# Sums over partitions for the adaLN blocks: ones-products and DRAM rows replaced by block transposes, row sums and one small product

## The chip, the cores and the metric

One Trainium2 chip, of which the kernel uses one core. The metric is the device time of one launch in microseconds; lower is better. The engines of the core run side by side and wait for each other through semaphores: TensorE (PE, with its weight loads as PEld) multiplies, VectorE (DVE), ScalarE (ACT) and GpSimd (POOL) work element by element, and SyncE (SP) issues every DMA of this kernel from one queue, in order.

## The reference

Two layers of a diffusion backbone for 640 tokens (128 context, 512 latent) of 1024 features, all in float32. Each layer mixes tokens through three branches (gated MLP, attention, RWKV-7), merges them, and then runs an MLP; each half is modulated by six vectors of 1024 values for each of two conditionings (the context's and the latent's):

```python
mod = (jax.nn.silu(cvec) @ P['w_ada'][l] + P['b_ada'][l])[:, None, :]
sh1, sc1, g1, sh2, sc2, g2 = jnp.split(mod, 6, axis=-1)
h = x * (1 + sc1) + sh1
...
x = _layer_norm(ALPHA * x + g1 * mixed, P['ln1_g'][l], P['ln1_b'][l])
h = x * (1 + sc2) + sh2
f = jnp.square(jax.nn.relu(h @ P['w_up'][l])) @ P['w_down'][l]
x = _layer_norm(ALPHA * x + g2 * f, P['ln2_g'][l], P['ln2_b'][l])
```

The change concerns `mod`: for each layer a product of two rows of 1024 with a 1024 x 6144 matrix, 24 MB of weights read once.

## The kernel before

Big products are made from float32r parts: a weight block of 128x512 is loaded (`raw`), ScalarE copies it to `hi`, VectorE subtracts to get `lo` (`split`, L240 to L242), and three products (hi hi, hi lo, lo hi) stand for one of float32. There are three buffers for each of `raw`, `hi` and `lo`, so the splits run a little ahead of the products.

The `mod` matrix is cut into 12 blocks of 512 columns a layer; block `cb` belongs to the vector `cb // 2`. The first four blocks of layer 0 are done at the start by TensorE (`ada_first`). The other 20 go through `ada_block` (L290): for each of eight k-tiles it loads 128x512 weights (`wada`) and adds weights times silu(c) to an accumulator of 128x512 for each of the two conditionings, on VectorE (L306, L308), or, for the six blocks of layer 0 that run before the MLP, half of it on ScalarE and GpSimd (L302, L304). What is left is a sum over the 128 partitions. There, at L309 to L322, two products with a column of ones (L315) put each conditioning's sum as one row of 512 on one partition, 0 or 64, of a PSUM bank; the bias is loaded as a row (L314), added on VectorE (L318), and the row goes to DRAM (L319). The two gate vectors (2 and 5) are later read from there as rows, broadcast to all partitions (`res_rows`). The shifts and scales (0, 1, 3, 4) are wanted with features on partitions: after the second block of a vector, one DMA for each conditioning gathers 1024 single values into the tile `mod0`, `mod1`, `mod3` or `mod4` of shape [128, 8, 2] (L322).

`ada_block` is a generator; each `next` does one k-tile. Two blocks run at the start, before the RWKV projections (`EARLY`); four in the gates and merge of layer 0, three steps for each step of those (L389 to L392); and 14 (two of layer 0, twelve of layer 1) in layer 0's MLP, three steps behind each up projection of 128 features and each down projection of 256 columns (L1216, L1243). The MLP of layer 1 has none. In the MLP the weights of a step lie in a tile `P` with two buffers, which the bias rows share; the accumulator is `acc`. Layer 0's gate vector 5 (the two first of the 14 blocks) is read before the last quarter of the same MLP, and layer 1's shift and scale 0 and 1 at its end.

Instructions are written in the order of this code, and a planner places them in each engine's queue when the program is built, by a simulated timeline; on the chip every engine runs its queue in that order.

Of the kernel before, what the change touches and what calls it, by code (L numbers as in the profile page):

```python
# [11 lines left out]
F32 = mybir.dt.float32  # L12
# [11 lines left out]
KT = D // 128  # L24
# [6 lines left out]
# emission order of the units' stages: those of the prologue, then those of a period  # L31
# [15 lines left out]
class Two(list):  # L47
    """Two PSUM banks for the first cut tokens and the others."""
    cut = HALF

    def of(self, h, x):
        """Part h of the tokens of x."""
        return x[:, self.cut:NTOK] if h else x[:, 0:self.cut]
# [5 lines left out]
class Net:  # L59
# [67 lines left out]
    # ---- weights: 256 KB blocks, each split into two float32r parts that sum to it exactly  # L127
    def wsplit(self, src, extra=False):
        """[128, 1024] of weights as two blocks of 512 columns."""
        return [self.whalf(src[:, 512 * i:512 * i + 512], extra) for i in range(2)]  # L130
# [15 lines left out]
    # out[128 features, 640 tokens] in two halves; w: (hi, lo) column slices, x: lists of (hi, lo)  # L146
    def mm_k(self, ps, w, k, x):
        """The products of one of eight k-tiles."""
# [16 lines left out]
    def fm_blocks(self, srcs, xs, first=0, pre=()):  # L165
        """The products of successive weight blocks; the first three by parts of the tokens when first."""
# [22 lines left out]
    # token-major: out[tt] = x[tt].T @ w, 256 columns, w blocks of 4 k-tiles  # L189
# [20 lines left out]
    def tm_last(self, srcs, xs, slots):  # L210
        """The last two column blocks, one token tile after the other; yields each tile's [128, 512]."""
# [24 lines left out]
    def ev(self, ps, t):  # L236
        """Pairs of views to evacuate ps into t [128, 640]."""
        return [(ps.of(h, t), ps.at(h)) for h in range(2)]
# [5 lines left out]
    def consts(self):  # L244
# [9 lines left out]
        c["silu32"] = self.const.tile([128, KT, 32], F32, name="silu32")  # L254
# [5 lines left out]
    def consts2(self, names):  # L260
# [13 lines left out]
        if "ident" in names:  # L274
            c["one"] = self.const.tile([128, 64], F32, name="one")
            nc.gpsimd.memset(c["one"], 1.0)
            c["neg"] = self.const.tile([128, 128], F32R, name="neg")
            nc.vector.tensor_scalar(c["neg"], c["ident"], 0.0, -1.0, ALU.mult, ALU.add)
# [10 lines left out]
    # ---- adaLN: mod = silu(c) @ w_ada + b_ada, a 512-column block at a time  # L289
    def ada_block(self, l, cb, acc, ws, tmp=None):  # L290
        """Columns 512 * cb on: products and sums on VectorE (with tmp, half of them on ScalarE and GpSimd),
        the sums over the partitions on TensorE, to DRAM as rows."""
# [16 lines left out]
        b = ws()  # L309
        ps = self.D("ada")  # L310
        ones = self.c["blk1"][:, 128:129]
        for s in range(2):
            p = slice(64 * s, 64 * s + 1)
            self.load(b[p], a["bada_r"][l:l + 1, 512 * cb:512 * cb + 512])  # L314
            nc.tensor.matmul(ps[p, :], ones, acc[:, s], start=True, stop=True)  # L315
        for s in range(2):
            p = slice(64 * s, 64 * s + 1)
            nc.vector.tensor_add(b[p], ps[p, :], b[p])  # L318
            self.load(self.modd[l][cb // 2][s:s + 1, 512 * (cb % 2):512 * (cb % 2) + 512], b[p])  # L319
        if cb % 2 and cb // 2 not in (2, 5):  # L320
            for s in range(2):
                self.load(self.lc[l][f"mod{cb // 2}"][:, :, s], self.modd[l][cb // 2][s].rearrange("(k p) -> p k", p=128))  # L322

    # ---- per-layer small parameters
# [23 lines left out]
    def scale_bias(self, l, sh, sc, g=None, b=None):  # L348
        """Per-feature scale and bias of x_hat * g + b followed by * (1 + sc) + sh."""
# [17 lines left out]
    def put_hT(self, hT, t, xt, sb, groups=(0, 1)):  # L367
        """Token tile t of the feature-major activations from xt [128 tokens, 1024]."""
# [21 lines left out]
    # ---- branch B  # L390
    def attn_proj(self, l, hT):
        """Normalised and rotated q and k, and v, token-major, to DRAM."""  # L392
# [6 lines left out]
        def tables(name):  # L399
            # cos * g and (signed sin) * g with the halves swapped  # L400
# [52 lines left out]
    def attn_core(self, l):  # L453
# [8 lines left out]
        for g in range(2):  # L462
# [21 lines left out]
            for t in range(NT):  # L484
# [11 lines left out]
                # the largest score of each query and head  # L496
# [19 lines left out]
                # keys on the partitions: scores less the maximum, exp, and the sums over V and 1;  # L516
                # heads 0 and 2 in the first 64 columns of the array, 1 and 3 in the others
# [25 lines left out]
    # ---- branch A  # L543
# [56 lines left out]
    # ---- branch C  # L600
    def pad_evac(self, raw, ps):
        """[128, 640] from PSUM into the zero-padded sequence layout [0 | 128 | 0 | 512 | 0]."""
# [8 lines left out]
    def shift(self, d, raw, mu, omu, dst):  # L611
        """dst(n0, n1) = the output's columns; f + mu * (neighbour - f)."""
# [30 lines left out]
    def rwkv(self, l, others):  # L643
        """The eight units, a stage at a time, with steps of the other work between the stages."""
# [28 lines left out]
    def gn(self, l, hp):  # L673
        """Group norm over each head's 64 values, per token; bonus and gate."""
# [15 lines left out]
        # feature-major: (gn * g + b + bonus) * gate  # L690
# [19 lines left out]
    def unit(self, l, hp, d):  # L710
        """Two heads (hp), one direction: the delta rule in chunks of 64 tokens, a stage at a time."""
# [15 lines left out]
        # decay and in-context learning rate, from float32r parts: those of the first rank-64 input as  # L727
        # [high ; low], of the second as [low ; high], against the high part of the weights, and high against low
# [55 lines left out]
        # squared key norms, and the bonus  # L784
# [21 lines left out]
        # token-major: X = [A | W ; 0 | V] per head, G = [key copies | r part] per head | a parts  # L806
        # blocks of a chunk: keys and r part of head 0, of head 1, then the a parts of both
# [21 lines left out]
        # the 32 x 32 diagonal blocks, one per partition: inverses by substitution  # L829
# [45 lines left out]
        # XA = [A0 | W0 ; W1 | A1], in X where its zeros come later  # L875
# [10 lines left out]
        # W = (a part of the keys) V  # L886
# [10 lines left out]
        # the a part becomes [T0 | 0 ; 0 | T1]  # L897
# [5 lines left out]
        # off-diagonal block: T2 L T1 (d = 0), T1 L T2 (d = 1); first-applied rows at a, then b  # L903
# [19 lines left out]
        # [A' | U0] = T [A | W]  # L923
# [7 lines left out]
        # per chunk: [P | Q] (new state from the old) and [R' | Y0] (outputs from the old state)  # L931
# [23 lines left out]
        # states: [S ; I] (even head), [I ; S] (odd head), for the two sequences  # L955
# [7 lines left out]
        for q in range(8):  # L963
# [4 lines left out]
            # new states, then outputs; the heads in the two halves of the array's columns  # L968
# [23 lines left out]
    # ---- gates from the input projection  # L992
# [12 lines left out]
    # ---- merge of the branches, output projection, residual and norm  # L1005
# [19 lines left out]
    def gated(self, l, j, dp, xs):  # L1025
        """(1 + tanh) * (branch j's projection) for two tiles of 128 features."""
# [13 lines left out]
    def merge_a(self, l):  # L1040
        """The first branch's part of the merge, without the banks and tiles that attention holds."""
# [36 lines left out]
    # ---- y = ALPHA * x + gate * f, layer norm; f comes in token-major blocks of 256 columns  # L1078
# [111 lines left out]
    def mlp(self, l, hT, xsrc, xdst, nxt, side):  # L1190
        """side: a generator whose steps are spread over the weight blocks."""
# [54 lines left out]
    def ada_first(self, g, wt):  # L1246
        """Half g of the first shift and scale, on TensorE: three parts of the rows at a time, in column groups of the array."""
# [19 lines left out]
    def ada_in(self, blocks, acc, ws):  # L1267
        """adaLN blocks with the given tiles."""
# [16 lines left out]
    def spread(self, main, n, side, m):  # L1285
        """The n steps of main, with the m steps of side spread over them."""
# [223 lines left out]
```

## Time and profile before

| | |
|---|---|
| time, three runs | 3008.99 us median (3006.35 to 3011.65) |
| profiled execution: span, first to last instruction | 3001.1 us |
| profiled execution's own time beside its span | not given by itself; the runs' median lies 7.9 us above the span |
| mean granted TensorE clock | 0.956 |
| busy: TensorE / VectorE / ScalarE / GpSimd | 94% / 67% / 46% / 23% |
| DMA | 378 MB in 331,255 packets, 158,111 of them under 512 B |

The profile is of one execution. "Busy" is the time in which an engine has an instruction running; a busy TensorE can still be waiting inside its pipeline, and the ends of its products are modelled, so a product's cost is better read from how far apart the instructions around it start. A float32 product appears as two records. A wait is put down to the instruction that released it. Lines are those of the kernel printed above; helpers such as `load` (L125) and `split` (L242) carry many different uses, told apart by the tile's name.

### The profile page before, as it was taken

The numbers are of one execution on the slowest core, as the hardware profiler recorded it, in microseconds if no ns is written. First come the engines' busy times: TensorE is split into PE (matmuls) and PEld (weight loads), VectorE is DVE, ScalarE is ACT, GpSimd is POOL, SyncE is SP. The second block draws the span as 40 slices with busy tenths as digits, with TensorE's granted clock in tenths as the row PEclk, the third lists the DMA queues.
The fourth block names the chain that finished last, engine by engine and source line by source line (L and its number), as shares of the span: only waits on it lengthen the run. The fifth ranks groups of instructions, "written<-read, shape, count | busy, mean of one in ns | idle before, by whom it ended". The sixth has DMA issues, their size and how long they took to land.

```text
span 3001.1 us, 56460 instructions
## 1 busy us (share of the span) xinstructions
PE 2818.7 (94%) x21264; PEld 2536.2 (85%) x21264; DVE 2014.4 (67%) x3824; ACT 1365.8 (46%) x3206; POOL 690.3 (23%) x867
## 2 busy tenths in 40 slices
PE   7989989999979999999989899899999998999998
PEld 5878868877758989999989788777778898999998
DVE  4697878768776776777574877887687467223346
ACT  3445655565562342332344456655555524442332
POOL 3241371312233210001140411723121024000011
PEclk8989979999989999999999898899999999999999
DMA  7533323332477344445335332333323672222242
GB/s 259 177 111 118 92 89 94 101 100 79 131 239 241 109 144 153 149 154 170 110 111 154 112 114 77 112 89 103 103 72 105 220 239 99 71 74 72 77 134 85
DMA packets 331255, 378.37 MB, mean 126 GB/s; under 512 B 158111, under 2 KB 180119, under 8 KB 330983
## 3 DMA queue, kind: packets, MB, share of 16 engines
q1 hardware_dynamic: 330983, 374.77, 40.0%
q8 instruction: 167, 2.74, 0.4%
q14 instruction: 105, 0.86, 0.1%
HBM read 306.83 MB, written 67.83 MB: 125 GB/s over the span
## 4 chain that ended last, share of the span: by engine, by line
PE 61%; DVE 19%; DMA 8%; ACT 5%; issue 4%; SPq 2%; POOL 1%; DVEq 0%; ACTq 0%; POOLq 0%
PE fm L163 18%; PE tm L207 17%; PE gl L163 7%; DVE Pm L860 4%; PE br L163 4%; DVE T L861 2%; PE tm L233 2%; SPq L125 2%; PE g L816 2%; DVE lo L242 2%; PE st L973 1%; DMA ab<-ad 1%; PE ada L315 1%; PE o L531 1%; ACT q1k L977 1%
## 5 line engine op out<-in xcount | busy, mean ns | idle before, releaser
L242 DVE TENSOR_TENSOR lo<-raw,hi 128x512 fp32r<-128x512 f32 x514 | 386.6, 754 | 401.6 <-ACT hi L241 389.8
L163 PE MATMUL fm<-h,hi 128*128 128x320 f32 (+1 forms) x2720 | 614.7, 315 | 11.1 <-ACT h L387 10.8
L241 ACT ACTIVATE hi<-raw 128x512 fp32r<-128x512 f32 x514 | 323.0, 630 | 608.3 <-PE tm L207 319.5
L163 PEld LDWEIGHTS fm<-h,hi 128*128 128x128 f32 x2720 | 461.8, 191 | 32.6 <-issue 13.7
L163 PE MATMUL fm<-h,lo 128*128 128x320 f32 (+2 forms) x1360 | 419.9, 314 | 7.9 <-DVE lo L242 7.9
L163 PE MATMUL gl<-h,hi 128*128 128x320 f32 x1536 | 382.9, 326 | 2.3 <-ACT f L1001 1.6
L163 PEld LDWEIGHTS gl<-h,hi 128*128 128x128 f32 x1536 | 265.7, 193 | 23.3 <-issue 10.8
L163 PEld LDWEIGHTS fm<-h,lo 128*128 128x128 f32 x1360 | 258.2, 191 | 12.7 <-DVE lo L242 9.1
L860 DVE TENSOR_TENSOR Pm<-T,ab 120x22 f32<-120x22 f32 (+30 forms) x434 | 248.6, 573 | 10.1 <-POOL ab L846 0.8
L163 PE MATMUL gl<-h,lo 128*128 128x320 f32 x768 | 247.6, 323 | 0.0
L308 DVE SCALAR_TENSOR_TENSOR acc<-P,c_sg,acc 128x512 f32<-128x512 f32 x196 | 143.1, 770 | 45.2 <-DMA P<-in_wada_dram 44.4
L1205 POOL TENSOR_TENSOR X<-X,e 128x512 f32<-128x512 f32 x8 | 11.5, 1442 | 678.7 <-DMA e<-modd 353.7
L207 PE MATMUL tm<-hi,h 128*128 128x256 f32 x800 | 160.4, 294 | 0.6 <-ACT f L434 0.6
L861 DVE TENSOR_REDUCE T<-Pm 120x11 f32<-120x22 f32 (+30 forms) x434 | 150.2, 346 | 9.6
L163 PEld LDWEIGHTS gl<-h,lo 128*128 128x128 f32 x768 | 147.6, 192 | 10.0 <-issue 5.3
L163 PE MATMUL br<-h,hi 128*128 128x320 f32 x512 | 128.0, 338 | 22.2 <-DVE f L1036 9.5
L977 ACT ACTIVATE q1k<-st,edge 64x64 f32<-64x64 f32 x320 | 98.6, 308 | 88.6 <-PE st L973 82.8
L207 PEld LDWEIGHTS tm<-hi,h 128*128 128x128 f32 x800 | 130.4, 196 | 5.1 <-ACT f L434 1.0
L207 PE MATMUL tm<-hi,L 128*128 128x256 f32 x720 | 131.8, 283 | 0.0
L533 POOL TENSOR_TENSOR P<-P,Q 128x512 f32<-128x512 f32 x64 | 85.7, 1339 | 164.8 <-PE o L531 75.5
L163 PEld LDWEIGHTS br<-h,hi 128*128 128x128 f32 x512 | 92.9, 205 | 32.0 <-issue 15.3
L207 PE MATMUL tm<-lo,h 128*128 128x256 f32 x400 | 116.7, 293 | 3.0 <-DVE lo L242 3.0
(553 smaller groups left out, 6922.4 us busy)
## 6 DMA issues: line engine op xcount, KB each, us to landing
raw<-in_win_f_dram SPq DMA_DIRECT2D x172, 256.0 KB
raw<-in_wup_dram SPq DMA_DIRECT2D x128, 256.0 KB
raw<-in_wdn_dram SPq DMA_DIRECT2D x128, 256.0 KB
P<-in_wada_dram SPq DMA_DIRECT2D x114, 256.0 KB
w<-rk SPq DMA_DIRECT2D x48, 321.5 KB
gate<-f SPq DMA_DIRECT2D x48, 320.0 KB
raw<-in_wbr_dram SPq DMA_DIRECT2D x48, 256.0 KB
Ld<-rk SPq DMA_DIRECT2D x64, 160.0 KB
```

The lines of the kernel that those rows point to most:

```text
L125: self.nc.sync.dma_start(out=out, in_=in_)
L163: nc.tensor.matmul(ps.at(h), w[:, c], ps.of(h, x), start=(k == 0 and p == 0), stop=(k == n - 1 and p == 2))
L207: nc.tensor.matmul(out[t], x[:, ts], w[:, c], start=(k == 0 and p == 0 and (alone or t < 2)), stop=(k == n - 1 and p == 2 and (alone or t ...
L233: nc.tensor.matmul(o, x[:, ts], w[:, c], start=(k == 0 and p == 0), stop=(k == n - 1 and p == 2))
L241: self.nc.scalar.activation(hi, x, AF.Copy)
L242: self.nc.vector.tensor_sub(lo, x, hi.bitcast(F32))
L308: nc.vector.scalar_tensor_tensor(acc[:, s], w, cs[:, k, s:s + 1], acc[:, s], ALU.mult, ALU.add)
L533: nc.gpsimd.tensor_tensor(out=den, in0=den, in1=PT, op=ALU.add)
L816: nc.tensor.matmul(pg[h][:, 128 * j:128 * j + 128], BK[pr, c0 + j].rearrange("p s t -> p (s t)"), RAV[pr, c0 + j, 0:2, :].rearrange("p s t ...
L860: nc.vector.tensor_tensor(out=Pm[:, :, 0:nj], in0=T[:, :, js], in1=Am[:, js, i].unsqueeze(1).to_broadcast([3 * NB, CG, nj]), op=ALU.mult)
L861: nc.vector.tensor_reduce(T[:, :, i:i + 1], Pm[:, :, 0:nj], AX.X, ALU.add)
L977: nc.scalar.activation(St[kr, s, h, :], p4[kr, s, h, :], AF.Copy, scale=edge[kr, cc:cc + 1])
```

## The change

The sum over partitions is made in another way, and the result arrives with features on partitions at once.

For each conditioning, VectorE transposes the accumulator [128, 512] in blocks of 32x32 and sums each run of 32 values along its row. That leaves 16 values a partition, in which partition p holds the sum over one group of 32 partitions for the feature that p's place in its group stands for; both conditionings together are `red` [128, 32]. One product with `sel` [128, 128], which is 1 where two partitions have the same place in their groups of 32, adds the four groups up and gives every partition group the full sum. Four additions of 32 partitions each pick the features that belong there, add the bias from the tile `bada` that is already on the chip, and write them to `mod0`, `mod1`, `mod3` or `mod4`. For the gate vectors they go to a small tile `gmod`, and two DMAs a block scatter 512 single values each to the DRAM rows that `res_rows` reads. The bias input by rows (`bada_r`) is gone.

Around it: `sel` is built once from the identity (one reduction and three copies on VectorE); `silu32` moves from a tile of its own to one of the two `q1k` slots. Comments and docstrings were dropped, so lines shift.

```diff
-        c["silu32"] = self.const.tile([128, KT, 32], F32, name="silu32")
+        c["silu32"] = self.S([128, KT * 32], "q1k", bufs=2).rearrange("p (k n) -> p k n", n=32)
...
         if "ident" in names:
+            c["sel"] = self.const.tile([128, 128], F32, name="sel")
+            s0 = c["sel"][:, 0:32]
+            nc.vector.tensor_reduce(s0, c["ident"].rearrange("p (g i) -> p i g", i=32), AX.X, ALU.add)
+            for q in range(1, 4):
+                nc.vector.tensor_copy(c["sel"][:, 32 * q:32 * q + 32], s0)
...
-        b = ws()
+        red = self.S([128, 2, 16], "red", bufs=1)
+        for s in range(2):
+            b = ws()
+            nc.vector.transpose(b, acc[:, s])
+            nc.vector.tensor_reduce(red[:, s], b.rearrange("p (j r) -> p j r", r=32), AX.X, ALU.add)
         ps = self.D("ada")
-        ones = self.c["blk1"][:, 128:129]
-        for s in range(2):
-            p = slice(64 * s, 64 * s + 1)
-            self.load(b[p], a["bada_r"][l:l + 1, 512 * cb:512 * cb + 512])
-            nc.tensor.matmul(ps[p, :], ones, acc[:, s], start=True, stop=True)
-        for s in range(2):
-            p = slice(64 * s, 64 * s + 1)
-            nc.vector.tensor_add(b[p], ps[p, :], b[p])
-            self.load(self.modd[l][cb // 2][s:s + 1, 512 * (cb % 2):512 * (cb % 2) + 512], b[p])
-        if cb % 2 and cb // 2 not in (2, 5):
+        nc.tensor.matmul(ps[:, 0:32], self.c["sel"], red.rearrange("p s j -> p (s j)"), start=True, stop=True)
+        j, kb = cb // 2, 4 * (cb % 2)
+        lc = self.lc[l]
+        rows = j in (2, 5)
+        dst = self.S([128, 4, 2], "gmod", bufs=2) if rows else lc[f"mod{j}"][:, kb:kb + 4, :]
+        p4 = ps[:, 0:32].rearrange("p (s k q) -> p k q s", s=2, q=4)
+        for q in range(4):
+            pr = slice(32 * q, 32 * q + 32)
+            nc.vector.tensor_tensor(out=dst[pr], in0=p4[pr, :, q, :], in1=lc["bada"][pr, 4 * cb:4 * cb + 4].unsqueeze(2).to_broadcast([32, 4, 2]), op=ALU.add)
+        if rows:
             for s in range(2):
-                self.load(self.lc[l][f"mod{cb // 2}"][:, :, s], self.modd[l][cb // 2][s].rearrange("(k p) -> p k", p=128))
+                self.load(self.modd[l][j][s, 128 * kb:128 * kb + 512].rearrange("(k p) -> p k", p=128), dst[:, :, s])
```

## Rows read from the trace of the kernel before

**Rows 1.** The page's busy totals: us, share of the span, instructions.

```profile
PE 2818.7 (94%) x21264; PEld 2536.2 (85%) x21264; DVE 2014.4 (67%) x3824; ACT 1365.8 (46%) x3206; POOL 690.3 (23%) x867
```

**Rows 2.** Busy by stretch: length, PE, PEld, DVE, ACT, POOL, clock, DMA share, GB/s.

```profile
50.00:104.00 54.00, 46.11 (x257) 39.70 (x256) 39.93 (x42) 28.57 (x60) 29.41 (x43) 0.91 0.65 208
810.00:945.00 135.00, 108.22 (x740) 91.28 (x741) 91.18 (x129) 66.78 (x161) 54.38 (x39) 0.87 0.72 235
1050.00:1450.00 400.00, 387.87 (x2755) 362.34 (x2754) 288.47 (x453) 133.89 (x237) 27.67 (x20) 0.98 0.49 156
1180.00:1242.50 62.50, 62.50 (x403) 57.29 (x401) 44.51 (x70) 28.33 (x52) 0.00 (x0) 1.00 0.49 152
1242.50:1302.00 59.50, 59.50 (x485) 57.49 (x485) 40.94 (x73) 11.00 (x18) 0.00 (x0) 1.00 0.44 143
1423.00:1450.00 27.00, 22.80 (x134) 20.43 (x133) 25.89 (x35) 8.29 (x14) 9.73 (x6) 0.94 0.59 195
2647.00:2703.50 56.50, 56.50 (x387) 56.50 (x387) 16.85 (x23) 27.24 (x50) 0.00 (x0) 1.00 0.21 71
```

**Rows 3.** Waits of TensorE, 1050 to 1450 us: total, times, longest.

```profile
PE fm L163 <- DVE lo L242: 4.2, 1, 4.2
...
PE ada L315 <- DVE acc L308: 0.4, 1, 0.4
```

**Rows 4.** TensorE in time, 40 to 106 us: start, us, in brackets idle before.

```profile
66.82 1.87 PE L315 MATMUL ada<-X,c_blk 128*1 128x512 f32 x2 [5.34 <-DVE X L308]
...
94.86 1.02 PE L315 MATMUL ada<-X,c_blk 128*1 128x512 f32 x2 [2.35 <-DVE X L308]
```

**Rows 5.** TensorE in time, 1164 to 1328 us: a joined and a split block end.

```profile
1164.77 1.03 PE L315 MATMUL ada<-acc,c_blk 128*1 128x512 f32 x4
1165.73 0.39 PE L207 MATMUL tm<-hi,e 128*128 128x256 f32 x1
...
1323.32 0.31 PE L163 MATMUL fm<-h,lo 128*128 128x320 f32 x1
1323.56 1.02 PE L315 MATMUL ada<-acc,c_blk 128*1 128x512 f32 x2
1324.50 0.56 PE L163 MATMUL fm<-h,hi 128*128 128x320 f32 x2
```

**Rows 6.** Busy time of line 315 alone, 1050 to 1450 us: PE, then PEld.

```profile
1050.00:1450.00 400.00, 23.48 (x56) 2.00 (x56) 0.98 0.49 156
```

**Rows 7.** TensorE in time, 1056 to 1062 us: transposes of `put_hT`.

```profile
1058.17 0.66 PE L378 MATMUL tr<-c_ident,y 128*128 128x128 f32 x4 [2.82 <-ACT y L1151]
```

**Rows 8.** VectorE's groups by line and shape: busy us, mean ns of one, idle before.

```profile
L538 DVE RECIPROCAL Q<-o 128x256 f32<-128x256 f32 x20 | 35.1, 1756 | 23.8 <-PE o L536 18.0 <-issue 5.6
L318 DVE TENSOR_TENSOR P<-ada,P 1x512 f32<-1x512 f32 x28 | 19.1, 683 | 12.3 <-PE ada L315 11.8
L306 DVE TENSOR_SCALAR acc<-P,c_sg 128x512 f32<-128x512 f32 x28 | 12.4, 483 | 4.9 <-DMA P<-in_wada_dram 4.5
L682 DVE TENSOR_REDUCE gmean<-Y 128x10 f32<-128x640 f32 x8 | 6.5, 812 | 0.1
...
L1264 DVE TENSOR_TENSOR mod<-ada,bada 128x8 f32<-128x8 f32 x4 | 0.7, 164 | 0.2 <-issue 0.2
```

**Rows 9.** Waits of VectorE, 1050 to 1450 us.

```profile
DVE acc L308 <- DMA P<-in_wada_dram: 44.4, 52, 2.7
```

**Rows 10.** Waits of VectorE, 1180 to 1242.5 us.

```profile
DVE acc L308 <- DMA P<-in_wada_dram: 7.1, 8, 2.0
```

**Rows 11.** SP's queue in time, 871 to 877 us: start, us, what is issued.

```profile
871.90 1.01 SPq L125 DMA_DIRECT2D mod<-modd  x2
872.95 2.33 SPq L125 DMA_DIRECT2D F<-in_wada_dram  x1
```

**Rows 12.** The chain that ended last, 800 to 985 us: start, us, what.

```profile
875.39 3.15 DMA part<-f
878.60 5.55 DMA f<-gate
```

More of the change, by code (lines that the diff above doesn't have):

```diff
@@ L1423, in pack @@
     o["wada"] = c(f("w_ada").reshape(dp, KT, 128, 12, 512).transpose(0, 3, 1, 2, 4))
-    o["bada_r"] = f("b_ada")
     o["bada_f"] = c(f("b_ada").reshape(dp, 48, 128).transpose(0, 2, 1))
```

## The prediction

> **What bounds the kernel now.** I read the busy totals first, then busy time by stage, then who waited for whom, then single stretches of the queues. TensorE is busy 94% of the span, VectorE 67% [rows 1]; a total hides stages with different limits, so the stages decide. In the first layer's MLP (1050 to 1450 us), where 14 of the 20 adaLN blocks lie, TensorE is busy 387.9 of 400 us and VectorE 288.5 [rows 2], and one TensorE wait there is longer than 4 us: 4.2 us for a `lo` split [rows 3]. So in this stage TensorE's own work is the time. The second layer's MLP, which carries no adaLN, passes one up projection in 56.5 us at full TensorE; the first layer's takes 62.5 us, also at full TensorE, with three block ends in it [rows 2]. Elsewhere it is mixed: during the first two blocks (50 to 104 us) TensorE idles for the accumulators of adaLN itself [rows 4], and in the merge (810 to 945 us, four blocks) it is busy 108 of 135 us with the DMA engines at 0.72 [rows 2] and waits for loads and stores.
>
> **The change, part by part.**
>
> *TensorE loses two 512-column products a block.* Each appears as two records. Where a product stands alone between `fm` products, two `fm` products, which otherwise follow each other at 56.5 / 387 = 0.15 us [rows 2], start 1.18 us apart [rows 5]: it costs 1.03 us, a block 2.06. Where both stand together, on output partitions 0 and 64, all four records pass in 0.96 us [rows 5]. Nine of the 14 blocks are of the first kind, five of the second: 9 x 2.06 + 5 x 0.96 = 23.3 us; the view of that line in the stage says 23.5 [rows 6], which I take. *It gains* one product with a 128x128 stationary and 32 columns. The nearest are the transposes of `put_hT`, 128x128 with 128 columns: four records in 0.66 us, the last one's 0.27 us of pipeline included [rows 7], so 0.13 us a record and 0.26 a block. Bounds: 0.1 and, as before, 1.03. Saved in the MLP: 23.5 - 14 x 0.26 = 19.9 us, on the engine that sets the time.
>
> *VectorE loses* two additions of 1x512 at 0.683 us [rows 8] and *gains* two transposes, two row sums and four additions of 32x8. The sum over 640 elements to 10 takes 0.812 us [rows 8]; for 512 that is 0.65 to 0.69, I take 0.67. The small addition out of PSUM takes 0.164 us [rows 8]. No row has a 32x32 transpose of 128x512: bounded by the quickest pass over as many elements, 0.483 us, and by the slowest per element, the reciprocal's 1.756 us for 256, so 3.5 us for 512 [rows 8]. I take 0.68, what the addition of 512 takes [rows 8], since most 512-element operations lie there. Net: 2 x 0.68 + 2 x 0.67 + 4 x 0.164 - 2 x 0.683 = +2.0 us a block (bounds +1.6 and +7.6), +28 us in the MLP.
>
> [...]
>
> *What hides it.* The MLP has 400 - 288.5 = 111.5 us without VectorE work. Less the 19.9 by which the stage shrinks, 91.6 remain for 28; but 44.4 of them are waits for adaLN's own loads [rows 9], which stand in VectorE's queue ahead of the splits, so the cover is thin. In the up projection of 1180 to 1242.5 us: 44.5 busy + 3 x 2.0 + 7.1 of such waits [rows 2, 10] = 57.6 us, against 62.5 - 5.2 (two split ends and one joined) + 0.8 = 58.1 us of TensorE. Half a microsecond is left, and the down projections (40.9 of 59.5 [rows 2]) catch up what slips. Where the cover is gone is the last stretch, 1423 to 1450 us, VectorE 25.9 of 27 [rows 2], where the residual's products pile onto adaLN's last blocks and the 4.2 us wait lies: two block ends more cost 4 us there. Another 2 us I put down to bursts of four operations (2.7 us) ahead of a `lo`. MLP: -19.9 + 6 = -14 us.
>
> *Waits.* The four additions wait on the product, as the two did before; behind them in VectorE's queue stand the splits. The product itself now waits for all of the sums, where the old first product waited for half of the accumulator; in the MLP TensorE waited 0.4 us for that [rows 3].
>
> *SP's queue.* Gone: 40 bias loads, 40 row stores, 12 gathers of 1,024 four-byte elements; added: 16 scatters of 512. In the merge the issue behind a pair of gathers takes 2.33 us, where its like takes 0.33 [rows 11]; with the stage's second pair 4 us of SP, and the store issued right behind it and the gate load after that stand on the chain, the latter ahead of TensorE's `br` products [rows 12]. There TensorE also loses about 7 us of products in a stretch where it is the limit in part, and VectorE (91 of 135 busy [rows 2]) gains 8. I take -3 (bounds -10 and +4).
>
> *Early blocks.* TensorE idled 5.3 and 2.35 us for the accumulators [rows 4]; now 2.7 us of transposes and sums come between, less 1.8 of products: 2 x 0.9. These two blocks are gate rows, so two pairs of scatters are new; by their element count, half the gathers', a pair delays SP by 1 us. I take +2 in all (bounds -1 and +6).
>
> [...] The trace shows the gathers' delay alone [rows 11]. If a pair of scatters held SP for 2 us like one of gathers, the early part would be +4.
>
> *Start.* `silu32` takes one of the two `q1k` slots until the last early product; state loads into both slots go out ahead of the first of adaLN's loads in SP's queue. 0 to +3, I take +0.5: nothing forces them to the head of the queue. The four small operations for `sel` stand where VectorE waits for the first products anyway; nothing.
>
> **Sum:** -14 - 3 + 2 + 0.5 = -14.5 us. The profiled execution's span is 3001.1 us; the median of the runs, 3009.0, is 7.9 above it, which I carry over as what lies around the span. Span 2986.6, time **2994.5 us**. Own range of this case: 2984 to 3002.
>
> **Rivals.**
> 1. *VectorE gives it back.* For: half a microsecond of cover in the up projections, and order on an engine is fixed when the program is built, so one late load holds every split behind it. Against: WB = 3 buffers let a split be late by a weight half, 56.5 / 16 = 3.5 us of products [rows 2]. If half of the 28 us comes through to TensorE instead of 6, 8 us more go: 3002.5; if the merge, whose VectorE work grows too, gains nothing, 3 more: 3005.5 us.
> 2. *Slower: the transpose is slow.* One mechanism: at a transpose of T us the net is 2T + 0.64. The up projection's cover ends at T = 0.8; with half of the excess caught up in the down projections, each further microsecond costs 14 us, and the sum turns positive at about T = 1.8. At the reciprocal's rate, T = 3.5, it is -14.5 + 38 = +23: 3032 us; at T = 2.5 3018, which I take. For: it is an operation that no row shows, on four-byte elements. Against: most VectorE operations here pass 512 elements in 0.48 to 0.75 us.
> 3. *More than I count.* The MLP returns the 19.9 whole, and the merge, freed of 20 small transfers and of gathers on its chain, 10: -28, 2981 us. For: a gate load stands ahead of its products on the chain [rows 12]. Against: VectorE's pile at 1423 us.
> 4. *It doesn't do what it says*: the product would still occupy TensorE for 1.03 us at 32 columns. Then 11 us less is saved in the MLP: 3005. Against: the transposes' 0.13 a record.
>
> **How the numbers follow.** About 0.2% of the time, 6 us, is what a measurement can tell from no change. Forecast 0.56; more than counted 0.13; VectorE gives back 0.13 and the long product 0.04; slower 0.14. Faster by over 6 us (below 3003): 0.56 + 0.13 and a little of the rest, 0.70; within: 0.16; slower: 0.14. Range: below rival 3's middle and up past rival 1, to 2979 and 3014, leaving out half of rival 3's lower side and most of rival 2.
>
> **What would show it.** Right: L315 gone at 1.03 us and a product of about 0.26 in its place; the up projections at 57 to 59 us, TensorE full; VectorE about 40 us busier over the span. Wrong: transposes above 0.8 us; TensorE waits for `lo` in the up projections; the first 110 us longer by more than 4; SP held over 2 us behind scatters.

## The result and the profile after

The changed kernel takes 3038.93 us (3029.29 to 3044.24, 4 runs) against 3010.32 us before (3006.35 to 3015.25, 4 runs): a ratio of 1.0093, 95% interval 1.0070 to 1.0116. It is 0.9% slower, where 2994.5 us was forecast with a range of 2979 to 3014. Its profiled execution took 3035.54 us, with a span of 3033.8: what lies around the span is 1.7 us, not the 7.9 us that I carried over. With the same 1.7 us the execution of before that I read took about 3002.8 us, less than all four runs above: it was one of the quicker ones, and stages compared with it show some 4 us more loss than the medians do.

The page's busy totals, which answer to [rows 1]:

```profile
PE 2803.1 (92%) x21224; PEld 2552.5 (84%) x21224; DVE 2028.2 (67%) x3948; ACT 1362.8 (45%) x3206; POOL 688.4 (23%) x867
```

TensorE is 15.6 us less busy and VectorE 13.8 us more, and the span is 33 us longer: TensorE, which set the time in the MLP, now waits more. VectorE's new groups by line and shape (busy us, mean ns of one, idle before):

```profile
L319 DVE STREAM_TRANSPOSE P<-acc 128x512 f32<-128x512 f32 x28 | 18.3, 689 | 0.0
L320 DVE TENSOR_REDUCE red<-P 128x16 f32<-128x512 f32 x28 | 17.8, 674 | 0.2
...
L312 DVE TENSOR_SCALAR acc<-P,c_sg 128x512 f32<-128x512 f32 x28 | 12.4, 484 | 27.9 <-DMA P<-in_wada_dram 27.9
...
L330 DVE TENSOR_TENSOR mod<-ada,bada 32x8 f32<-32x8 f32 x48 | 7.7, 161 | 1.8 <-PE ada L322 1.1
```

The prices came out as they were put: transpose 0.689 us (0.68), row sum 0.674 (0.67), small addition 0.161 (0.164). What is new in these rows stands at their end: a block's first product (L312) waits 27.9 us in all for its load, against 4.5 to 4.9 before [rows 8].

The product that takes the place of the old two (the view of its line: ns at least, median, at most):

```profile
L322 PE MATMUL ada<-red,sel x40: 190/273/403, 73.0 to 1479.4; 128*128 128x32 f32 x40
```

A record takes 0.27 us with its pipeline, like the transposes [rows 7], and not 1.03: rival 4 did not happen.

The same stretches as in [rows 2], found by the start of the same products (length, PE, PEld, DVE, ACT, POOL, clock, DMA share, GB/s): the early blocks, the first layer's MLP, and its up projection of 1180 to 1242.5 us.

```profile
50.00:115.00 65.00, 48.88 (x286) 46.48 (x285) 42.86 (x55) 28.71 (x60) 30.48 (x41) 0.89 0.71 171
1052.30:1484.40 432.10, 380.59 (x2730) 372.77 (x2729) 306.91 (x537) 133.83 (x237) 26.28 (x20) 0.95 0.49 144
1197.00:1262.00 65.00, 59.25 (x395) 57.14 (x394) 53.77 (x96) 26.67 (x48) 0.00 (x0) 1.00 0.52 159
```

The MLP takes 432.1 us, where 400.0 were measured before and 386 forecast. Matching the products over the whole span, the changed kernel is 10.7 us behind at 150 us, about 10 at 800, 2.4 at 1050, 34.4 at 1450 and 32.9 at the end. So two places lose: the early blocks and the MLP. The waits of TensorE in that MLP (total, times, longest), for [rows 3]; `fm` and `tm` are the products of the up and the down projections, `ada` those of the adaLN blocks:

```profile
PE tm L207 <- DVE lo L242: 19.4, 9, 8.9
PE fm L163 <- DVE lo L242: 18.4, 13, 7.3
...
PE ada L322 <- DVE red L320: 2.1, 1, 2.1
```

And why `lo` is late, in SP's queue (start, us, what is issued) and then in the chain that ended last (the work and the waits followed back from the end, one behind the other: start, us, what), around one gate block:

```profile
1103.85 0.93 SPq L125 DMA_DIRECT2D modd<-gmod  x2
1105.30 0.34 SPq L125 DMA_DIRECT2D P<-in_wada_dram  x1
```

```profile
1104.52 0.76 DVE acc L314
1105.30 10.82 DMA P<-in_wada_dram
...
1117.65 2.40 DMA P<-in_wada_dram
...
1134.77 9.74 DMA P<-in_wada_dram
...
1259.56 11.81 DMA P<-in_wada_dram
...
1273.54 1.65 PE tm L207 x6
```

The issue of the two scatters (`modd<-gmod`) keeps SP for 0.93 us only. But the load issued at 1105.30, right behind them, takes 10.82 us to land, where the same load takes 2.40 us a little later. VectorE stands at a block's product for it (up to 9.9 us), with the splits queued behind, and TensorE waits for `lo` (up to 8.9 us). The other two long landings stand behind scatters too (issued at 1131.52 and 1257.51). At the same places the kernel falls behind by steps: by the start of the same products it loses 8 us around the first pair and 12 around this third one. In the early blocks a load behind the first pair takes 8.51 us and one behind the second 11.33.

### The profile page after: what moved, and what is told of

Read it like the earlier page. It is cut to its first block, busy times and chain, and to the rows that moved or that the text cites. A ratio compares the mean times of both kernels' runs of the same rounds, so it can differ in the third digit from the quotient of the medians.

```text
span 3033.8 us, 56370 instructions
## 1 busy us (share of the span) xinstructions
PE 2803.1 (92%) x21224; PEld 2552.5 (84%) x21224; DVE 2028.2 (67%) x3948; ACT 1362.8 (45%) x3206; POOL 688.4 (23%) x867
## 4 chain that ended last, share of the span: by engine, by line
PE 52%; DVE 22%; DMA 15%; issue 4%; ACT 4%; SPq 1%; POOL 1%; DVEq 0%; ACTq 0%; POOLq 0%
PE tm L207 13%; PE fm L163 13%; PE gl L163 7%; DMA P<-in_wada_dram 5%; PE br L163 3%; DVE Pm L871 3%; DVE lo L242 2%; PE g L827 2%; PE tm L233 2%; DVE acc L314 2%; DVE T L872 2%; SPq L125 1%; PE st L984 1%; PE uA L163 1%; PE o L542 1%
## 5 line engine op out<-in xcount | busy, mean ns | idle before, releaser
L242 DVE TENSOR_TENSOR lo<-raw,hi 128x512 fp32r<-128x512 f32 x514 | 379.0, 739 | 399.6 <-ACT hi L241 387.0
L163 PE MATMUL fm<-h,hi 128*128 128x320 f32 (+1 forms) x2720 | 620.4, 318 | 27.3 <-ACT hi L241 14.6
L163 PEld LDWEIGHTS fm<-h,hi 128*128 128x128 f32 x2720 | 466.7, 194 | 35.3 <-ACT hi L241 15.6
L163 PE MATMUL gl<-h,hi 128*128 128x320 f32 x1536 | 370.3, 319 | 1.4 <-ACT f L1012 1.4
L163 PEld LDWEIGHTS gl<-h,hi 128*128 128x128 f32 x1536 | 259.6, 188 | 18.8 <-issue 8.0
L871 DVE TENSOR_TENSOR Pm<-T,ab 120x22 f32<-120x22 f32 (+30 forms) x434 | 240.0, 553 | 9.9 <-POOL ab L857 0.8
L207 PE MATMUL tm<-lo,L 128*128 128x256 f32 x360 | 103.5, 288 | 13.5 <-DVE lo L242 13.5
```

The lines of the kernel that those rows point to most:

```text
L163: nc.tensor.matmul(ps.at(h), w[:, c], ps.of(h, x), start=(k == 0 and p == 0), stop=(k == n - 1 and p == 2))
L207: nc.tensor.matmul(out[t], x[:, ts], w[:, c], start=(k == 0 and p == 0 and (alone or t < 2)), stop=(k == n - 1 and p == 2 and (alone or t ...
L242: self.nc.vector.tensor_sub(lo, x, hi.bitcast(F32))
L871: nc.vector.tensor_tensor(out=Pm[:, :, 0:nj], in0=T[:, :, js], in1=Am[:, js, i].unsqueeze(1).to_broadcast([3 * NB, CG, nj]), op=ALU.mult)
```

## Experiments

The medians beside each run are compared by the ratio to the kernel before on the same chip (medians of before: 3004 to 3012 us). Two ratios with intervals as wide as these can be told apart from some 7 us on; "costs nothing" below means less than that. MLP lengths are those of the first layer's, by the start of the same products, each in the one execution that was profiled: before 400, changed kernel 432. Of each edit the lines that matter are shown, `...` marks what is left out; where no other kernel is named, it is an edit of the changed kernel.

**1. Are the scatters the cost?** Theory S says so; theory V blames VectorE's added work and the load tiles that the transposes hold. Three variants of the changed kernel take the scatters away in different ways, and one adds them to the kernel before.

`s1_rows_pe`, rows of 512 bytes through a TensorE transpose:

```diff
...
+            nc.tensor.transpose(ps[0:8, 128:256], gm.rearrange("p s k -> p (s k)"), self.c["ident"])
+            gr = b[0:8, 0:128]
+            nc.vector.tensor_copy(gr, ps[0:8, 128:256])
...
-                self.load(self.modd[l][j][s, ...].rearrange("(k p) -> p k", p=128), dst[:, :, s])
+                self.load(self.modd[l][j][s, ...].rearrange("(k p) -> k p", p=128), gr[4 * s:4 * s + 4])
```

> The changed kernel, but the gate values go to DRAM as eight rows of 512 bytes (one small TensorE transpose and one copy per gate block) in place of the two scatters of 512 four-byte values; nothing else differs. Theory S (each pair of scatters keeps the DMA engines from the loads behind it for some 8 to 11 us, and the eight pairs cost the kernel about 30 us): loads behind the gate rows land in 2 to 4 us again, the first 110 us are within 4 us of the kernel before, the first layer's MLP is 10 us or more shorter than before, time about 2995 us (2988 to 3003). Theory V (VectorE's added work and the two load tiles that the transposes hold make the splits late, whatever the stores): the time stays above 3025 us and the long TensorE waits for lo stay in the MLP.

Measured: 2993.90 us, ratio 0.9948 (0.9931 to 0.9965). As S says, 45 us below the changed kernel. But the MLP took 404.5 us, not "10 us or more shorter than before": S is right for the whole and not for that stage, and this became the question of the second group.

`s2_gates_old`, the old code for the eight gate blocks:

```diff
+        if cb // 2 in (2, 5):
+            ...
+                nc.tensor.matmul(ps[p, :], ones, acc[:, s], start=True, stop=True)
+            ...
+            return
```

> The changed kernel, with the eight gate blocks computed the old way (two products of 512 columns, bias rows loaded, rows stored) and the other twelve the new way. Theory S: no scatter is left, so about 3000 us (2993 to 3008): the gain of twelve blocks less their products. Theory V: VectorE's added work shrinks by eight blocks of 20 only, so it stays above 3015 us.

Measured: 3001.59 us, 0.9965 (0.9951 to 0.9979), as S expects.

`s3_runs16`, 128 runs of 16 bytes a store:

```diff
...
-                self.load(self.modd[l][j][s, ...].rearrange("(k p) -> p k", p=128), dst[:, :, s])
+                self.load(self.modd[l][j][s, ...].rearrange("(p k) -> p k", k=4), gm[:, s])
```

> The changed kernel with the same number of DMAs at the same place behind the same waits, of the same 2 KB each, but each writes 128 runs of 16 bytes instead of 512 of 4 bytes; the values of the gate rows land in another order, so the output is not the reference's. Theory S, with the cost in the number of pieces: a quarter of the delay, about 2996 to 3005 us, loads behind it land in 3 to 6 us. If a store's cost were in its being a partial write of whatever size: above 3020. Theory V: above 3025 us, as the changed kernel.

Measured: 2994.43 us, 0.9950 (0.9930 to 0.9969). Same number of DMAs, same bytes, same place, same waits: the cost is gone, and its MLP took 399 us. That leaves the shape of the transfers alone; the source tile is laid out `[128, 2, 4]` here too, but `u4_scatter_dense` below has that layout and the whole cost.

`s4_before_scatter`, scatters added to the kernel before:

```diff
+        if cb // 2 in (2, 5):
+            for s in range(2):
+                self.load(self.scr[s, ...].rearrange("(k p) -> p k", p=128), self.lc[l]["bada"][:, 4 * cb:4 * cb + 4])
```

> The kernel before with two scatters of 512 four-byte values added behind each of its eight gate blocks, into a spare DRAM tile that nothing reads; otherwise unchanged. Theory S: slower than before by 20 to 45 us, with TensorE waits for lo behind the scatters. Theory V: within 6 us of before.

Measured: 3040.62 us, 1.0102 (1.0079 to 1.0125). The time agrees with S, the place does not: nothing held these scatters back, so all sixteen were issued between 27.9 and 92.2 us, the kernel was 35 us behind at 150 us, and its MLP took 401.2 us. It shows that sixteen scatters cost some 30 us at that place too, with nobody to read them, and nothing on the MLP.

**2. Why does the MLP gain nothing without scatters?** Theory H: both of the load tiles (`P` has two) are held by the transposes until the row sums are done, so the next block's first loads start late. Theory B: VectorE's added work itself.

`s5_psum`, on `s1_rows_pe` (the gate rows go through a load tile of their own):

```diff
-            b = ws()
+            b = ws() if tmp is not None else self.Sp("T")
             nc.vector.transpose(b, acc[:, s])
...
-            gr = b[0:8, 0:128]
+            gr = ws()[0:8, 0:128]
```

> s1_rows_pe, with the transposes of the MLP's blocks written into a free PSUM bank in place of adaLN's two load tiles. s1_rows_pe lost nothing to scatters, yet its first layer's MLP took 404.7 us against 400.0 before, where the prediction said 386. Theory H (the two load tiles are held by the transposes until the row sums are done, so the next block's loads start late: VectorE's waits for a block's first load are 17.6 us there against 4.5 before): these waits fall under 8 us, the MLP to 390 to 396 us, time about 2984 us. Theory B (VectorE's own added time, some 3.5 us in one piece at each block's end, makes the splits late): the MLP stays at 401 to 406 us, time 2990 to 2998 us.

`s6_no_transposes`, on `s1_rows_pe`, with the same change of `gr`:

```diff
-            b = ws()
-            nc.vector.transpose(b, acc[:, s])
+            b = acc[:, s]          # in the MLP's blocks alone
```

> s1_rows_pe with the transposes of the MLP's blocks left out (the row sums read the accumulator, so the second layer's shifts, scales and gates and the first layer's last gate are not the reference's). It holds no load tile and has 1.38 us less VectorE work a block. Theory H: as s5_psum within 4 us. Theory B: MLP 10 us or more below s1_rows_pe (395 or less) while s5_psum is not, time 2984 us or less.

`s7_rows_direct`, on `s5_psum`:

```diff
...
+            nc.tensor.matmul(ps[0:32, 0:32], red.rearrange("p s j -> p (s j)"), self.c["sel"][:, 0:32], start=True, stop=True)
+            nc.vector.tensor_add(gb, ps[0:32, 0:32], gb)      # gb: the bias as 32 rows of 32
...
+                self.load(self.modd[l][j][s, ...].rearrange("(j r) -> j r", r=32), gb[16 * s:16 * s + 16])
```

> s5_psum, with the gate blocks' product the other way round (the row sums stationary, the 0/1 matrix moving), so that the gate values come out as 32 rows of 32 in PSUM, and are stored as runs of 128 bytes after one addition: no transpose of the gate rows on TensorE and no wait for VectorE's additions in TensorE's queue (4.6 us in s1_rows_pe's MLP). Theory H and B: 3 to 6 us below s5_psum. If TensorE had waited there for nothing that counts: the same as s5_psum.

`s8_split_ends`, on `s7_rows_direct`:

```diff
             nc.vector.tensor_reduce(red[:, s], b.rearrange("p (j r) -> p j r", r=32), AX.X, ALU.add)
+            if tmp is None:
+                yield
```

> s7_rows_direct, with the end of an MLP block's work on VectorE in two steps: after each transpose and row sum the other work gets its turn. Theory B: the splits wait for half as long behind a block's end, 5 us or more below s7_rows_direct. Theory H: within 3 us of s7_rows_direct.

Measured: `s5_psum` 2970.02 us, 0.9884 (0.9866 to 0.9902); `s6_no_transposes` 2979.56, 0.9914 (0.9898 to 0.9931); `s7_rows_direct` 2970.46, 0.9884 (0.9866 to 0.9902); `s8_split_ends` 2976.52, 0.9912 (0.9889 to 0.9935). The MLP by stretch, first of `s1_rows_pe`:

```profile
1036.50:1441.00 404.50, 375.27 (x2732) 367.42 (x2733) 308.82 (x542) 133.57 (x237) 27.07 (x20) 0.97 0.48 154
```

then of `s5_psum`:

```profile
1041.00:1422.00 381.00, 369.52 (x2745) 366.32 (x2744) 307.88 (x536) 133.93 (x238) 27.67 (x20) 0.98 0.51 163
```

VectorE is as busy in both (308.8 and 307.9 us); the stage is 23.5 us shorter. Waits in the MLP of `s1_rows_pe`, TensorE's and VectorE's:

```profile
PE fm L163 <- DVE lo L242: 10.8, 11, 3.9
PE ada L333 <- DVE gmod L331: 4.6, 3, 2.1
PE tm L207 <- DVE lo L242: 3.4, 5, 1.4
```

```profile
DVE acc L314 <- DMA P<-in_wada_dram: 56.1, 55, 2.5
DVE acc L312 <- DMA P<-in_wada_dram: 17.6, 14, 2.1
```

and the same of `s5_psum`:

```profile
PE fm L163 <- DVE lo L242: 5.7, 3, 4.4
```

```profile
DVE acc L314 <- DMA P<-in_wada_dram: 26.8, 43, 2.3
...
DVE acc L312 <- DMA P<-in_wada_dram: 10.4, 5, 4.2
```

VectorE waits 36.5 us less for adaLN's loads, and TensorE's waits for `lo` shrink to what stood in the kernel before, 4.2 us at the end of the stage [rows 3], and a little more. Of the 19.9 us of products 19.0 come through (400.0 to 381.0). H holds, by more than it expected (2984), and B falls for `s5_psum`. Three points are left. `s7_rows_direct` took away a wait of 4.6 us and gained nothing by the ratio, nor in the MLP (380 us); 3 to 6 us would lie within the intervals, so this says little. `s6_no_transposes`, which holds no tile either and does less on VectorE, passed its MLP in 390 us, 9 us behind `s5_psum`, though H put them within 4: TensorE waits 10.9 us for `lo` there against 5.7, and why is open. `s8_split_ends` is not the test that it was meant to be: with two steps more a block, 26 of the 224 products and sums of the 14 blocks (nearly two blocks) run only behind the MLP, so its 378 us of MLP hold less work (VectorE 280 us busy against 304 in `s7_rows_direct`), and the whole is 8 us slower. Whether the length of VectorE's piece at a block's end matters is answered by `u3_transposes_twice` below.

**3. What of a scatter costs, and through what?**

`t1_psum_scatter`: the changed kernel with the edit of `s5_psum`.

> The changed kernel with its scatters, and the transposes of the MLP's blocks in a free PSUM bank (as s5_psum). If scatters and held load tiles add up (45 us between the changed kernel and s1_rows_pe, on top of s5_psum's 2970): about 3015 us. If the scatters' late loads cost the MLP time only because the held tiles leave no slack: the MLP stays under 388 us, and what is left of the 45 is the early blocks' share, some 17 us: 2984 to 2996 us.

`t2_scatter_act`:

```diff
-                self.load(self.modd[l][j][s, ...].rearrange("(k p) -> p k", p=128), dst[:, :, s])
+                nc.scalar.dma_start(out=self.modd[l][j][s, ...].rearrange("(k p) -> p k", p=128), in_=dst[:, :, s])
```

> The changed kernel with the scatters issued from ScalarE's queue instead of SP's. Theory E (the pieces occupy the DMA engines that all loads share): loads still land late, 3025 us or more. Theory O (only what stands behind them in SP's own queue is late): 3005 us or less.

`t3_runs16_x512`:

```diff
...
+            nc.gpsimd.tensor_copy(gm[:, :, :, 1:4], gm[:, :, :, 0:1].to_broadcast([128, 2, 4, 3]))
...
+                self.load(self.modd[l][j][s, 512 * kb:512 * kb + 2048].rearrange("(k p x) -> p k x", p=128, x=4), gm[:, s])
```

> The changed kernel with each scatter of 512 values of 4 bytes made one of 512 runs of 16 bytes (each value and three copies on GpSimd, into a DRAM tile four times as long; the residual reads its first quarter, so the output is not the reference's). Theory N (the cost goes by the number of pieces): 3025 us or more. Theory Z (it goes by the piece being 4 bytes): 3005 us or less, as the 128 runs of 16 bytes.

`t4_gathers`, on `s1_rows_pe`:

```diff
+            for s in range(2):
+                self.load(gm[:, s], a["wada"][l, cb, s, 0, 0:512].rearrange("(k p) -> p k", p=128))
```

> s1_rows_pe with two gathers of 512 four-byte values (reads of a weight row into the small gate tile, used by nothing) behind each gate block. If reading pieces costs what writing them does: s1_rows_pe + 30 to 45, 3024 to 3040 us. If only writes are dear: within 6 us of s1_rows_pe's 2994 us. The prediction's own price, 1 us of SP a pair, would give 2994 to 3002 us.

Measured: `t1_psum_scatter` 3021.11 us, 1.0030 (1.0014 to 1.0046): the two costs add up, 44 us above `s5_psum` by the ratios; that free tiles would absorb the late loads is refuted. Its MLP of 415 us, first, beside that of `s3_runs16`, will be wanted below:

```profile
1049.50:1464.50 415.00, 376.26 (x2728) 371.49 (x2727) 306.27 (x536) 133.50 (x237) 26.30 (x20) 0.95 0.52 150
```

```profile
1042.50:1441.50 399.00, 371.05 (x2725) 364.45 (x2726) 307.96 (x536) 133.75 (x237) 26.47 (x20) 0.98 0.50 156
```

`t2_scatter_act` 3049.59, 1.0140 (1.0098 to 1.0182): with the scatters on another queue the loads on SP's are as late (four of them land in 10.8 to 11.4 us in the MLP; in the 10 us from 1249.5 on 22 GB/s are moved), so standing behind them in one queue is not it. `t3_runs16_x512` 3007.59, 0.9991 (0.9974 to 1.0008): 13 us above `s1_rows_pe`, between both theories. `t4_gathers` 2994.52, 0.9950 (0.9936 to 0.9964): reading as many four-byte pieces costs nothing here by the time (its MLP took 409 us against the 404.5 of `s1_rows_pe`).

The last group adds stores to `s1_rows_pe`, into a DRAM tile that nobody reads. `u4_scatter_dense`:

```diff
+            for s in range(2):
+                self.load(self.scr[s].rearrange("(k p) -> p k", p=128), gm[:, s])
```

> s1_rows_pe (gate rows stored as rows of 512 bytes) with the changed kernel's two scatters of 512 four-byte values a gate block added, into a spare DRAM tile that nothing reads. If the scatter itself is the cost, whoever reads it: the changed kernel's 3039 us again (3030 to 3048). If the cost were the residual's loads waiting for the scattered rows: within 6 us of s1_rows_pe's 2994 us.

`u1_scatter_apart`, each value 512 bytes from the next:

```diff
+                self.load(self.scr[s].rearrange("(k p) x -> p k x", p=128)[:, :, 0], gm[:, s])
```

> u4_scatter_dense with the 512 values of a scatter 512 bytes apart in DRAM instead of side by side. Theory C (count: each four-byte piece is a partial write of its own): the same as u4_scatter_dense within 8 us. Theory L (pieces that fall on the same stretch of DRAM one behind the other wait for each other): within 10 us of s1_rows_pe, 3004 us or less.

`u2_quarter`:

```diff
+                self.load(self.scr[s, 0:128].rearrange("(k p) -> p k", p=128), gm[:, s, 0:1])
```

> u4_scatter_dense with a quarter of the pieces (128 four-byte values side by side a store). Theory C: a quarter of the cost, about 3005 us (3000 to 3012). Theory L: the same stretches are hit as often each, a quarter of them, so the same 3000 to 3012; under 3000 would say that the delay has a threshold.

`u3_transposes_twice`, on `s7_rows_direct`:

```diff
             nc.vector.transpose(b, acc[:, s])
+            if tmp is None:
+                nc.vector.transpose(b, acc[:, s])
```

> s7_rows_direct with each transpose of the MLP's blocks done twice: 1.38 us more VectorE a block, 19 us over the 14. If the prediction's cover holds (the up projections have half a microsecond left, half of the excess is caught up, a further microsecond a block costs 14 us): about 13 us more than s7_rows_direct, 2980 to 2988 us. If VectorE has room once the load tiles are free: within 5 us of s7_rows_direct's 2970 us.

Measured: `u4_scatter_dense` 3040.96 us, 1.0098 (1.0075 to 1.0120): the whole cost, with no reader. `u1_scatter_apart` 2996.72, 0.9949 (0.9932 to 0.9966): the same 512 four-byte writes, laid apart, cost nothing. Theory C falls, and L's forecast came true; that pieces on one stretch wait for each other is its explanation, which no run shows. `u2_quarter` 3029.80, 1.0058 (1.0038 to 1.0078): a quarter of the pieces still costs 33 of the 45 us, and its MLP took 437 us as that of `u4_scatter_dense` (438); both theories expected a quarter. So how close together the four-byte pieces fall counts for more than how many there are, which also fits the 16-byte runs, where four times fewer fall on a stretch. The number is not without weight either: of those runs 128 a store cost nothing (`s3_runs16`) and 512 cost 13 us. How long such a stretch is, and which part of the chip makes the pieces cost, no run tells; one distance alone was tried. `u3_transposes_twice` 2977.46, 0.9888 (0.9867 to 0.9909): 19 us more of VectorE's work cost 1 us by the ratio, and 2 us of its MLP (382 against 380), not 13.

One view shows the delay at the loads: 10 us from just behind the same pair of stores on (the third of the MLP; columns as above, the last two being DMA share and GB/s). In the changed kernel:

```profile
1259.00:1269.00 10.00, 5.61 (x44) 5.41 (x43) 2.60 (x4) 3.10 (x6) 0.00 (x0) 1.00 0.34 17
```

In `u4_scatter_dense`:

```profile
1254.50:1264.50 10.00, 7.66 (x64) 7.46 (x62) 1.95 (x4) 3.07 (x5) 0.00 (x0) 1.00 0.33 23
```

In `u1_scatter_apart`:

```profile
1225.00:1235.00 10.00, 10.00 (x86) 10.00 (x85) 6.97 (x12) 3.70 (x6) 0.00 (x0) 1.00 0.48 133
```

In `s1_rows_pe`:

```profile
1231.00:1241.00 10.00, 10.00 (x86) 10.00 (x85) 7.00 (x11) 1.90 (x3) 0.00 (x0) 1.00 0.53 169
```

In `t4_gathers`:

```profile
1235.00:1245.00 10.00, 10.00 (x85) 9.93 (x84) 8.89 (x14) 1.90 (x3) 0.00 (x0) 1.00 0.68 188
```

17 GB/s against 133 to 188, and TensorE busy 5.6 of 10 us. The trace's single DMA pieces say how: behind the first MLP pair of the changed kernel the 1,024 four-byte pieces are all passed within about 1 us, at 9 ns each, and look harmless. It is the 2 KB pieces of the loads behind them that take 0.34 us each on average for 10 us (counted from 1 us behind the stores' issue), up to 2.9 us, where 0.084 us is their median over the run. Over the six pairs of the MLP the mean is 0.14 to 0.50 us in the changed kernel and 0.11 to 0.12 in `u1_scatter_apart`, by the same count; the view above gives 0.12 there too (0.48 of 16 engines for 10 us, at 133 GB/s, in pieces of 2 KB).

## Why the prediction was wrong

**The step that failed** is that on the scatters, under "Early blocks": "by their element count, half the gathers', a pair delays SP by 1 us". SP's 0.93 us for the issue of a pair was right. The cost is at the loads, about 45 us over eight pairs (the changed kernel against `s1_rows_pe`, and `u4_scatter_dense` the other way round): 28 us or more in the MLP (432.1 against 404.5), where I had put down nothing, and 7 to 18 us in the early blocks (three pairs of kernels with and without scatters, at 150 us), where I had +2. I took the price from the gathers [rows 11], by element count. But reads cost nothing in `t4_gathers` (0.9950, against the 0.9948 of `s1_rows_pe`), and the rows of before hold no scatter of this kind at all: a new operation in a resource that every stage shares needed the wide bounds that I gave to the transpose.

The dearer price that I set beside it, a pair that holds SP for 2 us, made +4 of the early part's +2 and reached no other stage. Nor is the price just that the pieces are small: the four-byte writes that `u1_scatter_apart` (0.9949) adds to `s1_rows_pe` (0.9948) cost nothing, and the 128-byte ones of `s7_rows_direct` (0.9884, as `s5_psum`) don't either.

**The MLP's cover.** TensorE's saving was sized right: with the loads undisturbed the stage shrinks from 400.0 to 381.0 us (`s5_psum`), 19 of the 19.9 us. The give-back of 6 us was wrong in cause and size. I charged it to VectorE's 2.0 us a block; doubled transposes show that this work costs next to nothing once the tiles are free (2 us of MLP for 19 us more of it). What gives back 23.5 us (404.5 against 381.0) is a wait that I had in the rows and did not follow: of adaLN's two load tiles the old code held one at a block's end, the new code holds both, so the next block's first load is issued only after a row sum. In the changed kernel's chain (start, us, what):

```profile
1126.04 0.58 DVE red L320
...
1126.64 2.57 DMA P<-in_wada_dram
...
1129.23 0.89 DVE acc L312 x2
```

The 44.4 us of waits for those loads [rows 9] said that the loads have no slack. So the MLP reads: 400.0 - 19.0 + 23.5 + 27.6 = 432.1 us.

How the last 51 us divide depends on the runs that one compares, since `s1_rows_pe` brings work of its own: a product and a copy for each gate block, and a load tile that is held until the gate rows have been stored. `t1_psum_scatter` differs from the changed kernel by the transposes' destination alone, and its MLP is 17 us shorter (415 against 432); `s3_runs16` differs by the form of the stores, and its MLP is 33 us shorter (399). Held tiles so cost 17 to 24 us, and scatters 28 to 34. My up projection's sum has a slip besides: two split ends and a joined one are 5.1 us, not 5.2; nothing hangs on it.

**The other terms.** Early blocks without scatters come out 0 to 7 us ahead at 150 us, where I had +2.5 with the start; `s2_gates_old`, which computes them the old way, is 5.3 ahead, so it isn't the new form's doing. The merge (800 to 950 us) took some 9 us less in the changed kernel, where I had 3. But `s4_before_scatter`, which has the old merge, gained some 18 to 20 there on the kernel before, so what the change does to it is not separated.

**The rivals.** Rival 1 named the right place (half of the cover comes through to TensorE) with the wrong cause. Rival 2's slow transpose did not happen (0.69 us against 1.8 from which it decides). Rival 3's MLP, "the 19.9 whole", is what `s5_psum` measures. None had the way it went. That `s1_rows_pe` lands on 2993.9 us, next to the forecast, is chance: its MLP is 18 us above the forecast one.

Of the signs that were to tell it wrong, three came: TensorE's waits for `lo` in the up projection (5.8 us in eight waits; 59.25 us busy of 65.0), a first part longer by more than 4 us, and SP held over 2 us behind scatters. The last came at the fifth pair of the MLP, where the weight load behind it holds SP for 8.11 us; behind the other five no issue of that stage takes over 1.6 us:

```profile
1440.31 0.93 SPq L125 DMA_DIRECT2D modd<-gmod  x2
1441.28 1.93 SPq L125 DMA_DIRECT2D e<-modd  x4
1443.31 8.11 SPq L125 DMA_DIRECT2D raw<-in_wup_dram  x1
```

Of the signs that were to tell it right, the short product came, the up projections at 57 to 59 us did not, and VectorE is 13.8 us busier, not 40. The operations of the change do add 40 us by the sum of their durations (27.8 + 27.0 + 12.9 - 27.3), but products and splits of the same number and shape took 15 us less in the changed kernel, for a reason that is not shown, and what overlaps counts once in a busy total.

Two edits make the idea of the change pay: the transposes into an unused PSUM bank and the gate rows stored as runs (`s5_psum`, `s7_rows_direct`), 0.9884 of the time before, some 34 us.

## What to carry to other kernels

The price of a DMA was not its time in the issuing queue here (0.93 us for a pair of scatters, 10.82 us until the load behind it had landed): look at what lands next, on every queue, and give a form of store that no row shows bounds that reach to the stages it shares the engines with. Write feature-major values to DRAM through a form whose pieces are long, or at least not next to each other: rows of 512 bytes gave 0.9948 here, with 512 four-byte values a store added to them 0.9949 at 512 bytes apart and 1.0098 side by side. When a new step borrows a rotating tile (one of several buffers that are used in turn), ask which load was to go into that tile next, and when it may now start (23.5 us of MLP here); waits for these loads before the change (44.4 us here) say whether it has slack.

## What the hardware showed

I had not expected that 128 four-byte writes side by side delay the loads behind them nearly as much as 512 do (437 and 438 us of MLP, against 405), that 512 such writes laid 512 bytes apart cost nothing (0.9949 against 0.9948), that reads in four-byte pieces cost nothing (0.9950 against 0.9948), or that the scatter's own pieces look short in the trace (9 ns) while the 2 KB pieces of others stretch from 0.084 to as much as 2.9 us.
